# Four places in a hand-written TensorE order: two weighted sums and two heads' output transposes in an attention stage

## The chip, the cores and the metric

The kernel runs on one core of a Trainium2 chip. The metric is the device time of one execution in microseconds. Runs of the kernel before took 1316.26 to 1317.3 us, with a median of 1317.28.

## What is computed

The program is a two-layer decoder trunk for 512 tokens of width 1024, all in float32: a Mamba-2 mixer and a convolutional feed-forward layer, then differential attention and another feed-forward layer. The change is in the attention, whose reference is, cut to the core:

```
def block(args):
    qblk, i = args
    ...
    logits = jnp.einsum('bqhcd,bkhcd->bhcqk', qblk, k).astype(jnp.float32) * scale
    logits = logits + bias[None, :, None]
    logits = jnp.where(dist >= 0, logits, -jnp.inf)
    p = jax.nn.softmax(logits, axis=-1)
    attn = p[:, :, 0] - lam * p[:, :, 1]
    return jnp.einsum('bhqk,bkhd->bqhd', attn.astype(v.dtype), v)
...
o = rms_norm(o, subln_g) * (1.0 - lam_init)
return o.reshape(b, s, V_TOTAL) @ out_w
```

There are 8 heads. Each head has two query and key maps of 64 features (c = 0, 1) and one value of 128. The output of each head is normalised over its 128 features, and all heads go through one output projection.

## The kernel before

Every projection has its operands split into a rounded high half and a remainder, and three matmuls (high by high, high by low, low by high) make one product. The helper `mm3` (lines 207 to 210) does this for the output projection; `proj` (lines 1326 to 1349) does it for values and queries. Weights come by DMA, two pieces ahead of their use; ScalarE makes the high half (`wh`) and VectorE the low half (`wl`, line 174 or 159).

**Units.** Attention works in units (class `Unit`, line 1499). A head has three units, `PARTS`: query blocks 0 and 1, query block 2, query block 3, because of the causal mask. Units are numbered head_part, as in 4_0. Four operations make up the work on a unit:

- `logits` (lines 1509 to 1541): TensorE makes the logits of both maps into two PSUM banks; VectorE adds the bias and finds the row's extreme (line 1533) and so frees the bank; ScalarE takes the exponential (line 1540).
- `weigh` (lines 1543 to 1552): VectorE combines the two maps into one set of weights (line 1550).
- `turn` (lines 1554 to 1560): TensorE transposes the weights (line 1559), and ScalarE copies them out of PSUM (`at`, line 1560).
- `values` (lines 1562 to 1574): TensorE makes the weighted sum of the values (`po`, line 1570), with the transposed weights as the stationary operand, and ScalarE copies the result to `ot` (line 1573). After a head's last unit follows `normed_out` (lines 1576 to 1586): a square on ScalarE, a sum, a reciprocal root and the multiplication at line 1586 on VectorE.

A head that is normalised goes through `turned_out` (lines 1588 to 1599): four transposes on TensorE (`oT`, line 1592), a ScalarE copy that makes the high half (`oh`, line 1596) and a VectorE operation that makes the low half (`ol`, line 1597). The bank is free when both have read it.

**Banks.** PSUM has two pools of four banks. Logits, turned weights, weighted sums, output transposes and the transposes of queries (`ktq`, copied out as `qT` on ScalarE, line 1375) share the pool `aux`; projections use the pool `mm`.

**Order.** Only TensorE's order is written by hand (line 1647 opens a manual schedule for it). It is a list of strings, `ORDER` (line 1484), one row for each pair of units, read by the loop at lines 1687 to 1695:

- L: logits and weighing of the next pair of units
- f: the next step of a filler, a chain of generators (line 1653): values of heads 0 to 3, queries of heads 4 to 7, values of heads 4 to 7, then the first half of the output projection. Each has 16 steps of six matmuls with 512 columns, and ten of these steps run ahead of the list.
- a: `turn` of the next unit; v: `values` of the next unit; o: `turned_out` of the next normalised head

The order of instructions on ScalarE and VectorE is laid by the framework when the program is built. Each engine then runs its own in that order. One example of where this order differs from the code's: the normalising multiplications of the second query projection (`knq`, line 1361) are kept back by the code until the filler step f35.

Counted from zero, these are the steps around the change, as the list has them before:

```
row 4   L4(2_2,3_0) f31 f32 a7(2_1) v6(2_0) f33 v7(2_1) f34 o1 a8(2_2) f35
row 5   L5(3_1,3_2) f36 f37 a9(3_0) v8(2_2) f38 v9(3_0) a10(3_1) f39
row 7   L7(4_2,5_0) f44 f45 a13(4_1) f46 v12(4_0) f47 o3 a14(4_2) f48
row 8   L8(5_1,5_2) f49 f50 v13(4_1) a15(5_0) f51 v14(4_2) v15(5_0) a16(5_1)
row 10  L10(6_2,7_0) f56 f57 a19(6_1) v18(6_0) f58 v19(6_1) o5 a20(6_2)
row 11  L11(7_1,7_2) f59 f60 a21(7_0) v20(6_2) f61 v21(7_0) a22(7_1)
```

The steps f32 to f47 make the values of heads 4 to 7, token block by token block within each pair of input blocks. The copies of the finished values (`vt`, line 1480) are issued by f45 for the token blocks 0 and 1 and by f47 for the blocks 2 and 3. The transposes of the queries follow f36 and f37. The output projection's first half begins with f48.

After the list `last_out` (line 1627) does the last head's transposes and the second half of the output projection, and the second feed-forward layer (line 1699) follows.

Of the kernel before, what the change touches and what calls it, by code (L numbers as in the profile page):

```python
# [42 lines left out]
def trunk_kernel(ctx: ExitStack, tc, x, ssm_ln_g, ssm_in_w, ssm_conv_w, ssm_conv_b, ssm_dt_bias,  # L43
# [1249 lines left out]
    with tc.tile_pool(name="att", bufs=1) as ap, ExitStack() as later:  # L1293
# [184 lines left out]
        def vproj(key, i):  # L1478
            def evac(b, ps, rt):
# [17 lines left out]
        fl = lambda a: a.rearrange("p a b -> p (a b)")  # L1497
# [238 lines left out]
```

## Time and profile before

| What | Value |
|---|---|
| Runs | 1316.26, 1317.28, 1317.3 us |
| Profiled execution | 1317.05 us |
| Its span, first to last instruction | 1315.3 us |
| Mean granted TensorE clock | 1.000 |
| HBM traffic | 160.21 MB read, 6.44 MB written |

The profile names engines PE (TensorE matmuls), PEld (TensorE weight loads, which overlap PE), DVE (VectorE), ACT (ScalarE), POOL and SP. Times are microseconds from the span's start. In the timeline a row has the start, the duration, the engine, the line of the kernel, the operation, `out<-in` by tile names, the shape and a count; a square bracket has the idle time of the engine ahead of it and what ended that. Several like instructions in a row are merged into one. A float32 matmul whose operands aren't split shows as two instructions, so a weighted sum of three products shows as x6. The list of waits gives, for each pair of waiter and releaser, the total, the count and the longest. The attention stage with the list runs from about 803 to 940 us.

### The profile page before, as it was taken

What the parts mean: (1) busy time and instruction counts of PE and PEld (TensorE: products, weight loads), DVE (VectorE), ACT (ScalarE), POOL (GpSimd) and SP (SyncE); (2) the same over time, 40 slices, a digit from 0 to 9 for tenths busy, and PEclk for the clock granted to TensorE, in tenths of its full rate; (3) what the DMA queues carried; (4) which work ended last, traced back from release to release, by engine and by line L of the source; (5) the groups of instructions that cost most, each with busy time, mean ns of one, the idle gap of its engine ahead of it and who ended that gap; (6) DMA issues with size and microseconds to landing.
All of it is one profiled execution on the core that took longest, in us unless ns stands there. A gap on an engine that the chain in (4) does not pass through costs nothing.

```text
span 1315.3 us, 18265 instructions
## 1 busy us (share of the span) xinstructions
PE 1307.8 (99%) x6771; PEld 1096.2 (83%) x6771; DVE 1073.1 (82%) x1774; ACT 713.8 (54%) x1156; POOL 176.8 (13%) x244
## 2 busy tenths in 40 slices
PE   9999999999999999999999999999999999999998
PEld 8878888888888988898889887777888888888887
DVE  7989878888888877876888878677777978887886
ACT  6696554743344445544556667676654444544452
POOL 5230200300021401020113210000020100010001
PEclk9999999999999999999999999999999999999999
DMA  7453433432234657673766754222224445443635
GB/s 210 150 162 88 150 101 109 138 95 87 82 96 138 124 142 203 180 161 113 216 168 145 192 128 120 73 65 66 64 80 160 98 118 186 103 96 112 192 64 128
DMA packets 202552, 167.84 MB, mean 128 GB/s; under 512 B 7580, under 2 KB 175904, under 8 KB 202464
## 3 DMA queue, kind: packets, MB, share of 16 engines
q1 hardware_dynamic: 176080, 124.93, 31.8%
q0 software_dynamic: 22928, 36.46, 14.7%
q10 hardware_dynamic: 3456, 5.30, 1.1%
q8 instruction: 53, 0.87, 0.3%
q14 instruction: 35, 0.29, 0.1%
HBM read 160.21 MB, written 6.44 MB: 127 GB/s over the span
## 4 chain that ended last, share of the span: by engine, by line
PE 98%; ACT 1%; DVE 1%; issue 0%; DVEq 0%
PE ps_g L209 6%; PE ps_u L210 6%; PE ps_g L210 6%; PE ps_u L209 6%; PE ps_u L208 6%; PE ps_g L208 6%; PE ps_in L208 5%; PE ps_in L210 5%; PE ps_in L209 5%; PE ps_s L1239 3%; PE ps_s L1244 3%; PE ps_s L1242 3%; PE ps_s L1146 3%; PE ps_s L1141 3%; PE ps_s L1144 3%; PE ps_o L209 2%
## 5 line engine op out<-in xcount | busy, mean ns | idle before, releaser
L208 PE MATMUL ps_u<-xgh,wh_u 128*128 128x512 f32 x352 | 137.4, 390 | 0.0
L209 PE MATMUL ps_g<-xgl,wh_g 128*128 128x512 f32 x352 | 137.2, 390 | 0.0
L208 PE MATMUL ps_g<-xgh,wh_g 128*128 128x512 f32 x352 | 137.0, 389 | 0.0
L210 PE MATMUL ps_u<-xgh,wl_u 128*128 128x512 f32 x352 | 137.0, 389 | 0.0
L210 PE MATMUL ps_g<-xgh,wl_g 128*128 128x512 f32 x352 | 137.0, 389 | 0.0
L209 PE MATMUL ps_u<-xgl,wh_u 128*128 128x512 f32 x352 | 136.9, 389 | 0.0
L208 PE MATMUL ps_in<-xgh,wh_in 128*128 128x512 f32 x304 | 122.9, 404 | 0.0
L210 PE MATMUL ps_in<-xgh,wl_in 128*128 128x512 f32 x304 | 119.7, 394 | 0.0
L209 PE MATMUL ps_in<-xgl,wh_in 128*128 128x512 f32 x304 | 119.2, 392 | 0.0
L209 PEld LDWEIGHTS ps_g<-xgl,wh_g 128*128 128x128 f32 x352 | 66.0, 188 | 14.3 <-DVE xgl L488 0.7
L1244 PE MATMUL ps_s<-sl,wh_s 128*128 128x256 f32 x308 | 77.5, 283 | 0.0
L1242 PE MATMUL ps_s<-sh,wh_s 128*128 128x256 f32 x308 | 77.5, 283 | 0.0
L210 PEld LDWEIGHTS ps_g<-xgh,wl_g 128*128 128x128 f32 x352 | 66.1, 188 | 13.7
L209 PEld LDWEIGHTS ps_u<-xgl,wh_u 128*128 128x128 f32 x352 | 66.1, 188 | 13.6
L210 PEld LDWEIGHTS ps_u<-xgh,wl_u 128*128 128x128 f32 x352 | 66.0, 188 | 13.7
L208 PEld LDWEIGHTS ps_g<-xgh,wh_g 128*128 128x128 f32 x352 | 66.1, 188 | 13.6
L208 PEld LDWEIGHTS ps_u<-xgh,wh_u 128*128 128x128 f32 x352 | 66.1, 188 | 13.6
L1126 ACT ACTIVATE sh<-vg 128x256 fp32r<-128x256 f32 (+1 forms) x44 | 23.1, 524 | 99.1 <-DVE vg L1276 99.1
L1052 POOL DMA_DIRECT2D wz<-in_ffn_down_w_dram x36 | 44.2, 1290 | 235.2 <-DVE wl_s L1080 163.1
L1272 ACT ACTIVATE vg<-vg 128x512 f32<-128x512 f32 x44 | 27.8, 632 | 78.4 <-DVE vg L1024 78.3
L1024 DVE SCALAR_TENSOR_TENSOR vg<-ug,cf,vg 128x511 f32<-128x511 f32 x88 | 65.8, 747 | 5.5 <-ACT vg L1022 4.1
L1024 DVE SCALAR_TENSOR_TENSOR vu<-uu,cf,vu 128x511 f32<-128x511 f32 x88 | 65.7, 747 | 2.8 <-ACT vu L1022 1.4
(425 smaller groups left out, 3465.0 us busy)
## 6 DMA issues: line engine op xcount, KB each, us to landing
wr_g<-in_ffn_up_w_dram SPq DMA_DIRECT2D x44, 512.0 KB, 3.9
wr_u<-in_ffn_up_w_dram SPq DMA_DIRECT2D x44, 512.0 KB, 3.9
wr_in<-in_ssm_in_w_dram SPq DMA_DIRECT2D x40, 512.0 KB, 3.9
wz<-in_ffn_down_w_dram POOLq DMA_DIRECT2D x27, 512.0 KB, 5.8
m<-cumd POOLq DMA_DIRECT2D x16, 512.0 KB, 4.7
wr_out<-in_ssm_out_w_dram SPq DMA_DIRECT2D x16, 512.0 KB, 3.5
wr_s<-in_ffn_down_w_dram SPq DMA_DIRECT2D x13, 512.0 KB, 3.9
xT<-in_ffn_down_w_dram SPq DMA_DIRECT2D x10, 512.0 KB, 7.2
```

The source lines that it names most:

```text
L208: pe.matmul(ps, wh, xh, start=start, stop=False)
L209: pe.matmul(ps, wh, xl, start=False, stop=False)
L210: return pe.matmul(ps, wl, xh, start=False, stop=stop).ins
L1024: dve.scalar_tensor_tensor(out=v[:, s:], in0=u[:, :T - s], scalar=col(2 - s), in1=v[:, s:], op0=ALU.mult, op1=ALU.add)
L1052: pool.dma_start(view(t, nq), source(p0, c, nq, j, i), accum_op=ALU.add)
L1141: pe.matmul(pss[b], h, ws[q][1][:, cols], start=False, stop=end and q == qs[-1], skip_group_check=more)
L1144: pe.matmul(pss[b], h, ws[q][0][:, cols], start=first and q == qs[0], stop=False, skip_group_check=more)
L1146: pe.matmul(pss[b], w, ws[q][0][:, cols], start=False, stop=False, skip_group_check=more)
L1239: pe.matmul(v[:, b], wl[:, q, cols], h, start=False, stop=q == nq - 1, skip_group_check=not opens or b > 0)
L1242: pe.matmul(v[:, b], wh[:, q, cols], h, start=opens and q + b == 0, stop=False, skip_group_check=not opens or b > 0)
L1244: pe.matmul(v[:, b], wh[:, q, cols], w, start=False, stop=False, skip_group_check=not opens or b > 0)
L1272: act.activation(ga, ga, AF.Silu)
```

## The change

Three rows of the list differ, in four places. In row 4 the weighted sum v7 stands behind f34 instead of ahead of it. In row 7 the weighted sum v12 stands behind f47, and head 3's output transposes o3 stand ahead of f47. In row 10 head 5's output transposes o5 stand ahead of f58 and v19. The same steps are done in every row, and no operation is added or removed.

```
-                 "L f f a v f v f o a f",
+                 "L f f a v f f v o a f",
                  "L f f a v f v a f",
                  "L f f a v f v o a f",
-                 "L f f a f v f o a f",
+                 "L f f a f o f v a f",
                  "L f f v a f v v a",
                  "L f f a v f v o a f",
-                 "L f f a v f v o a",
+                 "L f f a v o f v a",
                  "L f f a v f v a",
                  "f a v f o v")
```

## The prediction

> **What bounds the kernel now.** The page comes first: the busy shares and the chain of work that ended last.
>
> ```profile
> PE 1307.8 (99%) x6771; PEld 1096.2 (83%) x6771; DVE 1073.1 (82%) x1774; ACT 713.8 (54%) x1156; POOL 176.8 (13%) x244
> PE 98%; ACT 1%; DVE 1%; issue 0%; DVEq 0%
> ```
>
> TensorE holds 98% of the chain. A place in its order is worth something only where it waits, so the next views are its busy time in stretches of the attention stage, and its own waits between 800 and 950 us.
>
> ```profile
> 840.00:860.00 20.00, 18.63 (x107) 14.48 (x106) 15.55 (x52) 16.39 (x45) 0.00 (x0) 1.00 0.22 66
> 860.00:880.00 20.00, 19.65 (x115) 15.38 (x116) 14.97 (x49) 14.63 (x40) 0.00 (x0) 1.00 0.22 66
> 880.00:900.00 20.00, 19.35 (x109) 14.66 (x108) 12.69 (x38) 13.23 (x33) 0.00 (x0) 1.00 0.20 67
> PE po L1570 <- ACT at L1560: 1.7, 1, 1.7
> PE po L1570 <- ACT vt L1480: 0.7, 1, 0.7
> ```
>
> The columns of a stretch are its start and end, its length, then PE, PEld, DVE, ACT and POOL busy, the granted clock and the DMA load. The clock is 1.00 throughout. TensorE has two holes, both in front of weighted sums (po, line 1570): one waits for a ScalarE copy of turned weights (at, line 1560), one for a ScalarE copy of values (vt, line 1480). To place them among the steps I read the timeline. Counting in the fixed list, I number the steps from zero: f34 is the 35th fill step, v7 the eighth weighted sum, o1 the second head's output transposes, a8 the ninth turn, L5 the sixth pair of logits.
>
> **The change, part by part.** Fill steps here are six matmuls of 512 columns; a weighted sum is a few matmuls and one ScalarE copy; an output transpose is four transposes, a ScalarE copy (oh) and a VectorE subtraction (ol). The fill steps that change places issue no DMA, and f47 alone has copies behind it (two of vt). So nothing moves past a DMA in SP's or POOL's queue.
>
> First, f34 ahead of v7.
>
> ```profile
> 857.00 0.47 PE L1335 MATMUL ps_v<-wh_v,xgh 128*128 128x512 f32 x1
> 858.24 0.40 PE L1337 MATMUL ps_v<-wh_v,xgl 128*128 128x512 f32 x1
> 859.83 0.47 ACT L1560 ACTIVATE at<-at 128x384 f32<-128x384 f32 x1
> 860.35 0.94 PE L1570 MATMUL po<-vt,at 128*128 128x128 f32 x6 [1.72 <-ACT at L1560]
> 861.04 0.48 PE L1335 MATMUL ps_v<-wh_v,xgh 128*128 128x512 f32 x1
> 862.52 0.60 PE L1592 MATMUL oT<-ident,ot 128*128 128x128 f32 x4
> ```
>
> f33 runs from 857.00, v7 at 860.35, f34 from 861.04, o1 at 862.52. A fill step takes 862.52 - 861.04 = 1.48 us, so v7 could have started at 857.00 + 1.48 = 858.48 and waits 1.87. The copy it waits for ends at 860.30 and stands in ScalarE's queue, which the edit leaves alone ahead of v7. With f34 in the hole TensorE is busy until 857.00 + 2.96 = 859.96, v7 still starts at 860.35, takes 861.04 - 860.35 = 0.69, and o1 follows at 861.04: **1.48 us earlier**. The upper end is 1.87, if that copy came earlier too.
>
> [...]
>
> What is late next? Behind o1 come a8, f35 and L5, and these rows set the pace:
>
> ```profile
> 862.43 1.89 DVE L1361 TENSOR_TENSOR knq<-knq,ssq 128x512 f32<-128x512 f32 x3
> 863.16 0.69 ACT L1596 ACTIVATE oh<-oT,c 128x512 fp32r<-128x512 f32 x1 [1.44 <-PE oT L1592]
> 864.24 0.74 DVE L1597 SCALAR_TENSOR_TENSOR ol<-oT,c,oh 128x512 fp32r<-128x512 f32 x1
> 864.88 1.77 PE L1527 MATMUL lg<-kT,qT 64*128 64x384 f32 x8
> 866.59 0.50 PE L1335 MATMUL ps_v<-wh_v,xgh 128*128 128x512 f32 x1
> 865.83 0.56 DVE L1533 CUSTOM_DVE_ANT_0 lg<-lg,tb 128x384 f32<-128x384 f32 x1 [0.17 <-PE lg L1527]
> 866.31 0.75 DVE L174 SCALAR_TENSOR_TENSOR wl_v<-wr_v,c,wh_v 128x512 fp32r<-128x512 f32 x1
> 868.06 0.75 DVE L174 SCALAR_TENSOR_TENSOR wl_v<-wr_v,c,wh_v 128x512 fp32r<-128x512 f32 x1
> 868.73 0.68 DVE L1533 CUSTOM_DVE_ANT_0 lg<-lg,tb 128x512 f32<-128x512 f32 x1
> 866.43 0.62 ACT L1540 ACTIVATE lg<-lg,mx 128x384 f32<-128x384 f32 x1
> 869.45 0.72 ACT L1540 ACTIVATE lg<-lg,mx 128x512 f32<-128x512 f32 x1 [0.46 <-DVE mx L1533]
> 870.17 2.40 ACT L1375 ACTIVATE qT<-ktq,c 128x512 f32<-128x512 f32 x4
> 871.58 0.61 PE L1570 MATMUL po<-vt,at 128*128 128x128 f32 x4
> ```
>
> VectorE is full from 862.43, with query multiplications (knq, line 1361) whose start no edit moves. Two things hang on its order, which the build lays and the old trace only hints at. (a) o1's bank is freed by ol. New, oh would run from 861.04 + 0.64 = 861.68 to 862.37 (0.64 is 863.16 - 862.52), so ol can start at 862.4, level with the first knq. L5 would start at 863.40; the third of its four banks, asked for 768 of 1792 columns in (0.73 of its 1.71 us, an estimate), is wanted at 864.13. With ol first or second on VectorE it is free by 863.8 and costs nothing; with ol still behind three knq it ends at 864.98 and costs 0.85. (b) L5's four reductions (line 1533) now have two weight subtractions of 0.75 among them, since a bank was not full yet when VectorE asked. New, all four are ready when VectorE is done with ol and four knq (2.52 + 0.74, near 865.6). Taken back to back they end near 867.9 instead of 869.41; the four exponentials (0.62, 0.62, 0.72, 0.72) then end near 868.9 instead of 870.17, the second of the four qT copies (0.6 each) near 870.1 instead of 871.4. v8 takes that copy's bank and has only 0.2 us to spare now (871.58 against 871.4); it would start near 870.2, **1.38 us earlier**. If both subtractions stay where they are, the reductions end only 0.2 earlier and v8 0.35. The code issues L5's reductions ahead of those subtractions, so I take 1.38; ends 0.35 and 1.87.
>
> Second, o3 and then f47 ahead of v12.
>
> ```profile
> 890.32 0.68 DVE L1586 TENSOR_TENSOR ot<-ot,so 128x512 f32<-128x512 f32 x1
> 892.66 0.61 PE L1570 MATMUL po<-vt,at 128*128 128x128 f32 x4
> 893.19 0.67 ACT L1480 ACTIVATE vt<-ps_v,tr_nkv 128x512 f32<-128x512 f32 x1
> 893.92 0.49 PE L1570 MATMUL po<-vt,at 128*128 128x128 f32 x2 [0.65 <-ACT vt L1480]
> 894.16 0.47 PE L1335 MATMUL ps_v<-wh_v,xgh 128*128 128x512 f32 x1
> 895.63 0.60 PE L1592 MATMUL oT<-ident,ot 128*128 128x128 f32 x4
> 896.42 0.48 PE L208 MATMUL ps_ao<-oh,wh_ao 128*128 128x512 f32 x1
> 921.88 0.83 PE L1570 MATMUL po<-vt,at 128*128 128x128 f32 x6
> 922.47 0.47 PE L208 MATMUL ps_ao<-oh,wh_ao 128*128 128x512 f32 x1
> ```
>
> Now v12, f47, o3 and a14 take 896.42 - 892.66 = 3.76. Without a wait they take: v12 0.59 (a sum of the same shape, 922.47 - 921.88), f47 895.63 - 894.16 = 1.47, o3 and a14 together 896.42 - 895.63 = 0.79: 2.85, a gain of **0.9**. Is the wait really gone? v12 would start near 892.66 + 0.44 + 1.47 = 894.57 (0.44 for o3 is an estimate, over half of the 0.79); the copy it needs ends at 893.86, and at 894.55 if o3's own copy (0.69, as above) went ahead of it on ScalarE. Both are in time. o3 needs head 3 normalised, which ends at 891.00, 1.66 before 892.66. Behind the moved v12, ScalarE's ot copy and a14 come later than the vt copies, and have f48 and L8 as cover. Ends: 0 and 0.9; it is nearest to the upper, since both producers are done.
>
> Third, o5 ahead of f58 and v19, with a20 left next to L11.
>
> ```profile
> 920.74 0.69 DVE L1586 TENSOR_TENSOR ot<-ot,so 128x512 f32<-128x512 f32 x1
> 925.58 2.32 PE L1527 MATMUL lg<-kT,qT 64*128 64x384 f32 x8
> 925.97 0.75 DVE L1597 SCALAR_TENSOR_TENSOR ol<-oT,c,oh 128x512 fp32r<-128x512 f32 x1 [0.96 <-ACT oh L1596]
> 927.83 0.50 PE L208 MATMUL ps_ao<-oh,wh_ao 128*128 128x512 f32 x1
> ```
>
> L11 takes 927.83 - 925.58 = 2.25, where L5, with the same four tiles, takes 866.59 - 864.88 = 1.71: 0.54 lost inside a step that the list of waits shows as busy, because a bank is held until ol ends at 926.72 and ScalarE's at copy stands behind o5's oh. Moved, o5 starts at 922.47, its oh and ol are done before 925.58, and the **0.54** goes; ends 0 and 0.54. o5's own input is ready at 921.43, 1.04 ahead.
>
> The sum: 1.38 + 0.9 + 0.54 = 2.8 us. Later stages have TensorE alone in the chain, so I carry it to the end. The profiled execution took 1317.05 us (span 1315.3); less 2.8 that is 1314.25. The median of the runs shown, 1317.28, lies 0.23 above it, so the forecast is **1314.5**. About 0.2% (2.6 us) is what a measurement of this kernel can tell from no change, and the sum stands just above it.
>
> **The rivals.** *VectorE's order stays* (0.22): the subtractions remain between L5's reductions and v8 waits for the qT copy; the first edit leaves 0.35, the sum is 1.8, the time 1315.5. For it: v8's 0.2 us of margin. Against it: VectorE ran ol, which was ready at 863.85, right after the knq it was then in, so its order follows readiness. *The waits move on* (0.12): copies are laid anew on ScalarE, and one edit pays while the others are taken back behind it; about 0.7, 1316.6. This includes a v12 that waits as before. *The copy comes earlier* (0.09): ScalarE's at for v7 moves up and the first edit gives 1.87; 3.3, 1314.0. *The early transposes wait* (0.07), the slower case: head 3's and head 5's normalisations run late, and o3 and o5, which now stand ahead of fill steps, hold TensorE. If they come L us later relative to TensorE than now, that costs (L - 1.66) + (L - 1.04); from L = 2.75 it eats the whole 2.8, at 3.0 it gives 1317.8, and from 4.1 it is slower by over 0.2%. Against it: that needs four more VectorE operations of 0.75 ahead of each.
>
> **How the numbers follow.** The forecast has 0.50. Its own spread is about 2.2 to 3.2 us, and some seven tenths of it lies above 2.6; with the earlier copy that makes faster 0.35 + 0.09 = 0.44. Slower is the tail of the last rival, 0.04; the rest, 0.52, is no change that can be told. The range runs from 1313.6, past the earlier copy, to 1316.6, through the two smaller gains; the forecast alone would have 1314.1 to 1315.1. Beyond it lie the slower case and half of the case that moves on.
>
> **What would show it.** After the change: no wait over 0.6 us at v7, o1 directly behind it; L5 at its 1.71; the two wl_v subtractions behind the last of L5's reductions; v8 1.2 to 1.5 earlier against f33; v12 without a hole in the middle; L11 at 1.7. It is wrong if v8, o3 or o5 shows a new wait, or if the PE busy time from 840 to 900 still lacks over 1 us.

## The result, and the profile after

The changed kernel took **1314.61 us** (median; 1313.80 to 1315.50) beside 1316.91 us of the kernel before on the same chip: a ratio of 0.9981, 95% interval 0.9975 to 0.9987, 2.30 us by the medians. Timed once more, beside another set of runs of the kernel before, it was 1314.82 against 1316.63, a ratio of 0.9986 (0.9977 to 0.9994), or 1.81 us. The forecast was 1314.5, with a sum of 2.8 us and a range from 1313.6 to 1316.6. The profiled execution took 1314.37 us with a span of 1312.7. Two executions of the experiments below took 1867.12 us (e2_row7) and 2663.43 us (e5_o1_first); the ratios leave them out, the medians hold them.

First the chain on the page of the changed kernel.

```profile
PE 99%; ACT 1%; DVE 0%; issue 0%; DVEq 0%
```

Then the three stretches of the attention stage, with the columns as before (start:end, length, PE, PEld, DVE, ACT, POOL, clock, DMA), and TensorE's own waits from 780 to 950 us, of which one is left.

```profile
840.00:860.00 20.00, 19.73 (x112) 15.46 (x112) 15.83 (x53) 16.68 (x46) 0.00 (x0) 1.00 0.20 65
860.00:880.00 20.00, 19.93 (x119) 15.65 (x120) 15.91 (x52) 15.00 (x42) 0.00 (x0) 1.00 0.22 66
880.00:900.00 20.00, 20.00 (x111) 15.34 (x111) 14.00 (x44) 14.68 (x37) 0.00 (x0) 1.00 0.28 93
```

```profile
PE po L1570 <- ACT at L1560: 0.3, 1, 0.3
```

TensorE is busy for 59.66 of these 60 us; before it was 57.63. The clock is 1.00 in both, so the 2.03 us are holes that closed. The third edit lies outside the window, at 920 us, and closes lost time inside a step.

The two profiled executions don't stand at the same place when the first edit comes: f33 starts at 856.72 here and at 857.00 before. So I measure from f33, which no edit moves, to o7, the last head's transposes behind the list (943.93 before, 941.23 after): 86.93 against 84.51, **2.42 us** gained inside the stage.

Now the three places. The timeline of the changed kernel around the first edit:

```profile
856.72 0.47 PE L1335 MATMUL ps_v<-wh_v,xgh 128*128 128x512 f32 x1
860.07 0.94 PE L1570 MATMUL po<-vt,at 128*128 128x128 f32 x6 [0.35 <-ACT at L1560]
860.85 0.60 PE L1592 MATMUL oT<-ident,ot 128*128 128x128 f32 x4
861.88 1.29 DVE L1361 TENSOR_TENSOR knq<-knq,ssq 128x512 f32<-128x512 f32 x2
863.10 0.74 DVE L1597 SCALAR_TENSOR_TENSOR ol<-oT,c,oh 128x512 fp32r<-128x512 f32 x1
863.21 1.81 PE L1527 MATMUL lg<-kT,qT 64*128 64x384 f32 x8
864.95 0.50 PE L1335 MATMUL ps_v<-wh_v,xgh 128*128 128x512 f32 x1
865.91 0.74 DVE L174 SCALAR_TENSOR_TENSOR wl_v<-wr_v,c,wh_v 128x512 fp32r<-128x512 f32 x1
867.19 0.68 DVE L1533 CUSTOM_DVE_ANT_0 lg<-lg,tb 128x512 f32<-128x512 f32 x1
867.87 0.73 DVE L174 SCALAR_TENSOR_TENSOR wl_v<-wr_v,c,wh_v 128x512 fp32r<-128x512 f32 x1
868.73 2.39 ACT L1375 ACTIVATE qT<-ktq,c 128x512 f32<-128x512 f32 x4
870.03 0.97 PEld L1570 LDWEIGHTS po<-vt,at 128*128 128x128 f32 x8 [0.21 <-ACT qT L1375]
870.03 1.16 PE L1570 MATMUL po<-vt,at 128*128 128x128 f32 x8
870.94 0.47 PE L1335 MATMUL ps_v<-wh_v,xgh 128*128 128x512 f32 x1
```

v7 is 3.35 behind f33, as before: its copy did not come earlier, and 0.35 of the wait is left. o1 follows v7 by 0.78, where before it came 2.17 behind (862.52 less 860.35): **1.39** gained. L5 takes 1.74 (1.71 before) and ol was laid in front of the third knq, so the bank of o1 costs next to nothing. One of the two weight subtractions stays among L5's reductions (865.91), the other went behind the last of them (867.87). The first knq starts 861.88 - 856.72 = 5.16 behind f33; before it was 862.43 - 857.00 = 5.43. The reason lies on ScalarE, where the second step of the reciprocal root that knq needs (ssq, line 500) stood behind v7's copy (line 1573). In the kernel before:

```profile
861.32 0.28 ACT L1573 ACTIVATE ot<-po 128x128 f32<-128x128 f32 x1
861.50 0.22 ACT L500 ACTIVATE ssq<-ssq 128x32 f32<-128x32 f32 x1
```

In the changed kernel it stands ahead of that copy, which starts at 861.08:

```profile
860.94 0.23 ACT L500 ACTIVATE ssq<-ssq 128x32 f32<-128x32 f32 x1
```

v8 is released by the second qT copy (868.73, two copies of 0.6), and its weights load only then, at the same moment as its first matmul; before, they were 0.11 ahead. The list of TensorE's waits doesn't show this one. v8 stands 870.03 - 856.72 = 13.31 behind f33, before 871.58 - 857.00 = 14.58: 1.27. The step after it, f38, stands 870.94 - 856.72 = 14.22 behind f33, and stood 15.39 behind it in the kernel before, by this row of its timeline:

```profile
872.39 0.48 PE L1335 MATMUL ps_v<-wh_v,xgh 128*128 128x512 f32 x1
```

So **1.17** leaves this place. The second edit, in the timeline of the changed kernel:

```profile
888.86 0.68 DVE L1586 TENSOR_TENSOR ot<-ot,so 128x512 f32<-128x512 f32 x1
891.20 0.60 PE L1592 MATMUL oT<-ident,ot 128*128 128x128 f32 x4
891.74 0.68 ACT L1480 ACTIVATE vt<-ps_v,tr_nkv 128x512 f32<-128x512 f32 x1
893.02 0.83 PE L1570 MATMUL po<-vt,at 128*128 128x128 f32 x6
893.97 0.75 DVE L1597 SCALAR_TENSOR_TENSOR ol<-oT,c,oh 128x512 fp32r<-128x512 f32 x1 [0.89 <-ACT oh L1596]
894.04 0.47 PE L208 MATMUL ps_ao<-oh,wh_ao 128*128 128x512 f32 x1
895.61 1.79 PE L1527 MATMUL lg<-kT,qT 64*128 64x384 f32 x8
```

v12 shows as one step of six matmuls without a hole; the copy it needs is done at 892.42. The four steps from o3 to f48 take 894.04 - 891.20 = 2.84, forecast 2.85, before 3.76. o3 starts 1.66 behind the end of its normalisation (889.54). ol3 ends at 894.72, ahead of L8 at 895.61. The third edit:

```profile
922.62 0.74 DVE L1597 SCALAR_TENSOR_TENSOR ol<-oT,c,oh 128x512 fp32r<-128x512 f32 x1
923.27 1.92 PE L1527 MATMUL lg<-kT,qT 64*128 64x384 f32 x8
925.12 0.50 PE L208 MATMUL ps_ao<-oh,wh_ao 128*128 128x512 f32 x1
```

L11 takes 925.12 - 923.27 = 1.85, before 2.25, forecast 1.7: **0.40** gained. ol ends at 923.36, 0.09 after L11 has begun: its oh is done at 922.06, but VectorE has been in two weighings (line 1550) since 921.95 and comes to ol only at 922.62. What that does inside the step is seen in the view of line 1527 over its first 0.25 us (columns: count; shortest, median and longest in ns; starts of the first and the last). First L5, then L11.

```profile
L1527 PE MATMUL lg<-kT,qT x2: 587/587/587, 863.2 to 863.2; 64*128 64x384 f32 x2
```

```profile
L1527 PE MATMUL lg<-kT,qT x2: 587/587/587, 923.3 to 923.4; 64*128 64x384 f32 x2
```

In L5 the matmuls of the two maps start together (each uses 64 of the rows); in L11 the second map starts 0.15 later (923.42 in the trace, against 923.27), when ol has given back its bank, and stays behind to the end. That is the 0.14 that is missing to 0.54.

### The profile page after: what moved, and what is told of

Read it like the earlier page. It is cut to its first block, busy times and chain, and to the rows that moved or that the text cites. A ratio compares the mean times of both kernels' runs of the same rounds, so it can differ in the third digit from the quotient of the medians.

```text
span 1312.7 us, 18264 instructions
## 1 busy us (share of the span) xinstructions
PE 1307.3 (100%) x6771; PEld 1096.3 (84%) x6771; DVE 1073.9 (82%) x1774; ACT 713.9 (54%) x1156; POOL 177.1 (13%) x244
## 4 chain that ended last, share of the span: by engine, by line
PE 99%; ACT 1%; DVE 0%; issue 0%; DVEq 0%
PE ps_g L209 6%; PE ps_u L208 6%; PE ps_g L208 6%; PE ps_u L210 6%; PE ps_g L210 6%; PE ps_u L209 6%; PE ps_in L208 5%; PE ps_in L210 5%; PE ps_in L209 5%; PE ps_s L1239 3%; PE ps_s L1244 3%; PE ps_s L1242 3%; PE ps_s L1146 3%; PE ps_s L1141 3%; PE ps_s L1144 3%; PE ps_o L209 2%
## 5 line engine op out<-in xcount | busy, mean ns | idle before, releaser
L1021 DVE TENSOR_TENSOR uu<-ps_u,nr_f 128x512 f32<-128x512 f32 x44 | 30.4, 690 | 48.0 <-PE ps_u L210 48.0
```

What stands on the lines that cost most here:

```text
L1021: dve.tensor_tensor(out=u, in0=ps, in1=r, op=ALU.mult)
```

## The experiments

All distances are from f33 to o7 in the profiled execution; the medians stand beside runs of the kernel before on the same chip.

| Kernel | f33 | o7 | Distance | Against before | Median, before's | Ratio (95%) |
|---|---|---|---|---|---|---|
| before | 857.00 | 943.93 | 86.93 | | | |
| changed | 856.72 | 941.23 | 84.51 | -2.42 | 1314.61, 1316.91 | 0.9981 (0.9975 to 0.9987) |
| e1_row4 | 856.31 | 942.11 | 85.80 | -1.13 | 1315.88, 1316.79 | 0.9993 (0.9984 to 1.0002) |
| e2_row7 | 856.25 | 942.30 | 86.05 | -0.88 | 1316.04, 1316.79 | 0.9992 (0.9983 to 1.0001) |
| e3_row10 | 857.73 | 944.27 | 86.54 | -0.39 | 1316.67, 1316.79 | 0.9998 (0.9989 to 1.0007) |
| e4_sum_only | 856.46 | 943.12 | 86.66 | -0.27 | 1316.85, 1316.79 | 0.9998 (0.9989 to 1.0007) |
| e5_o1_first | 856.91 | 941.43 | 84.52 | -2.41 | 1314.43, 1317.07 | 0.9980 (0.9971 to 0.9988) |
| e6_a20_first | 856.87 | 941.40 | 84.53 | -2.40 | 1314.07, 1317.07 | 0.9978 (0.9969 to 0.9986) |
| e7_o3_early | 857.45 | 946.35 | 88.90 | +1.97 | 1319.14, 1317.07 | 1.0013 (1.0004 to 1.0021) |
| e8_knq_pool | 857.16 | 942.33 | 85.17 | -1.76 | 1315.34, 1317.07 | 0.9987 (0.9978 to 0.9995) |
| e10_changed_again | 856.42 | 940.90 | 84.48 | -2.45 | 1314.82, 1316.63 | 0.9986 (0.9977 to 0.9994) |
| e11_a20_again | 857.42 | 941.95 | 84.53 | -2.40 | 1314.62, 1316.63 | 0.9982 (0.9973 to 0.9991) |

**Each row alone.** The theory: the three edits are worth what each is worth alone. The rival: one pays, and the others only move its wait.

```
e1   -"L f f a v f v f o a f"   +"L f f a v f f v o a f"     (row 4)
e2   -"L f f a f v f o a f"     +"L f f a f o f v a f"       (row 7)
e3   -"L f f a v f v o a"       +"L f f a v o f v a"         (row 10)
```

> Only v7 behind f34 (row 4); the other two rows as before. Theory (each edit removes its own wait, and what it gains is carried to the end by TensorE alone): v7 still waits, 0.3 to 0.5 us instead of 1.7; o1 is 1.4 us earlier than in the kernel before, v8 1.2 earlier since it then waits for the bank that the second qT copy frees, and 1.2 stays to the end: the time falls by 1.2 us. The hole in v12 stays 0.8. Rival (the edits pay only together): the gain is taken back at the hole in v12, which grows to 2.0, and the time is that of the kernel before.

> Only row 7: o3 ahead of f47, v12 behind it. Theory: v12 runs without a hole, f48 starts 0.86 us earlier than in the kernel before, the 1.7 wait at v7 stays, and the time falls by 0.9 us. Rival (the edits pay only together): without the earlier start that row 4's edit gives, ScalarE is as far behind at this place and v12 waits for the values all the same; under 0.3 us.

> Only row 10: o5 ahead of f58 and v19. Theory: L11 takes 1.85 us instead of 2.25 since its bank no longer waits for ol, and the rest up to 1.71 is the wait for the copy of a20 right ahead of it; a21 starts 0.4 us earlier than in the kernel before; the time falls by 0.4 us. Rival (a20 alone holds L11): nothing, L11 stays at 2.25.

The distances are 1.13, 0.88 and 0.39 shorter, together 2.40 of the 2.42. The waits of TensorE show it too: with row 4 alone the wait at v12 stands untouched beside the rest of v7's,

```profile
PE po L1570 <- ACT vt L1480: 0.7, 1, 0.7
PE po L1570 <- ACT at L1560: 0.3, 1, 0.3
```

and with row 7 alone the wait at v7 does:

```profile
PE po L1570 <- ACT at L1560: 1.7, 1, 1.7
```

The edits are independent, and the rival falls. In e3_row10 L11 takes 1.85, as expected; whether the rest is a20's copy, as the expectation has it, is tried further down. Each alone is too small for the runs (every interval holds 1); the traces tell.

**Row 7 with v12 moved and o3 left behind it.** Is o3's move needed, or only v12's? The other rows are those of the kernel before.

```
-"L f f a f v f o a f"
+"L f f a f f v o a f"
```

> Row 7 with v12 behind f47 but o3 left behind v12, where it was: the place of the weighted sum alone. Theory: f47 by itself covers the wait (v12 would start 1.4 us later than in the kernel before, 0.2 us after the values' copy ends), o3's move is worth nothing here, f48 0.86 us earlier as with both, time 0.9 less. Rival: the 0.2 us is too little, since ScalarE's copies are laid anew; v12 keeps a hole of 0.3 to 0.5 and the gain is 0.4 to 0.6.

The kernel was 0.27 better than the kernel before, not 0.88, and neither theory gave that. v12 has no hole here either, but the timeline shows what came in its place:

```profile
894.71 1.06 ACT L148 ACTIVATE wh_ao<-wr_ao 128x1024 fp32r<-128x1024 f32 x1
896.48 2.38 PE L1527 MATMUL lg<-kT,qT 64*128 64x384 f32 x8
896.94 0.74 DVE L1597 SCALAR_TENSOR_TENSOR ol<-oT,c,oh 128x512 fp32r<-128x512 f32 x1
897.74 0.29 PEld L1527 LDWEIGHTS lg<-kT,qT 64*128 64x128 f32 x2 [0.29 <-DVE ol L1597]
898.79 0.50 PE L208 MATMUL ps_ao<-oh,wh_ao 128*128 128x512 f32 x1
```

o3 now comes as late as 894.12. A weight copy of 1.06 us (wh_ao) is laid ahead of its oh on ScalarE, and on VectorE the subtraction that belongs to that copy (line 159, 1.23 us from 895.80) is laid ahead of its ol. So ol ends only at 897.68, 1.2 after L8 has begun; L8 waits for that bank and takes 898.79 - 896.48 = 2.31 where the changed kernel's takes 1.71 (897.32, the start of f49 there, less 895.61). In the changed kernel ol3 ended 0.9 ahead of L8 (894.72 against 895.61). So o3's move is worth 0.6 of the second edit's 0.88: it gives the bank back in time. This is the rival of waits that move on, in one edit left half done.

**o1 ahead of v7.** 0.35 of v7's wait is left; o1 could fill it.

```
-"L f f a v f f v o a f"
+"L f f a v f f o v a f"     (row 4 of the changed kernel)
```

> The changed kernel, with o1 ahead of v7 too (row 4: f33 f34 o1 v7), to fill the 0.35 us that v7 still waits. Theory (past v7 it is VectorE's query multiplications, then the qT copies on ScalarE, that set v8): L5 starts 0.4 to 0.5 us earlier than in the changed kernel, v8 at most 0.2 earlier, the time moves by 0.0 to 0.2. Rival (TensorE's order alone sets the pace): v8 and everything behind it 0.4 to 0.5 earlier, time 0.45 less.

In the trace L5 starts 6.05 behind f33 (862.96), in the changed kernel 6.49 (863.21), as the theory had it. Then come, in its timeline:

```profile
868.93 2.40 ACT L1375 ACTIVATE qT<-ktq,c 128x512 f32<-128x512 f32 x4
870.22 0.97 PEld L1570 LDWEIGHTS po<-vt,at 128*128 128x128 f32 x8 [0.26 <-ACT qT L1375]
```

v8 loads its weights 870.22 - 856.91 = 13.31 behind f33, to the hundredth where it does in the changed kernel. The qT copies start 12.02 behind f33 in this kernel and 12.01 in the changed one. v7's last wait is worth nothing: behind it the chain knq, reductions, exponentials, qT copies sets the time, and moving TensorE's steps ahead of it doesn't move it (the first knq is 5.17 behind f33 here, 5.16 in the changed kernel).

**a20 ahead of v19.** Can L11 come down to 1.7?

```
-"L f f a v o f v a"
+"L f f a v o f a v"     (row 10 of the changed kernel)
```

> The changed kernel, with a20 ahead of v19 (row 10: o5 f58 a20 v19), so that a weighted sum stands between a20 and L11. Theory (L11's remaining 0.14 us is the wait for the copy of a20's bank): L11 takes 1.71 us, a21 is 0.14 earlier, the time is 0.1 less, which only the trace can show. Rival (some bank is always late by so much, whichever step stands last): v19's copy holds L11 in its place, 1.85 or more.

> The changed kernel once more, as the neighbour of the next run. Theory: 2.4 us of gain in the trace, so a median 1.9 to 2.6 us under the kernel before.

> The changed kernel with a20 ahead of v19 in row 10, timed beside the changed kernel. Theory: its trace ended where the changed kernel's did (2.41 against 2.43 us early), so the 0.5 us by which its median was lower does not come back: the two medians lie within 0.4 us of each other. Rival: the places are worth 0.5 us that one profiled execution did not show; its median is again 0.4 us or more lower.

In the trace of the first run:

```profile
922.79 0.74 DVE L1597 SCALAR_TENSOR_TENSOR ol<-oT,c,oh 128x512 fp32r<-128x512 f32 x1
923.45 1.91 PE L1527 MATMUL lg<-kT,qT 64*128 64x384 f32 x8
925.29 0.50 PE L208 MATMUL ps_ao<-oh,wh_ao 128*128 128x512 f32 x1
```

L11 takes 1.84 again: ol ends at 923.53, 0.08 behind L11's start. So it is ol that holds L11, neither a20's copy nor v19's, and the reason given for the rest of L11 in e3_row10's expectation was wrong. The distance is the changed kernel's within 0.02. Its median had come out 0.5 lower, though, so the two were timed side by side, and there they are 0.20 apart (1314.82 and 1314.62), with intervals that overlap for the most part. No kernel of this study beats the changed one by what the runs can tell.

**o3 two fill steps too early.** What does a wait of early transposes, the slower rival, cost?

```
-"L f f a f o f v a f"
+"L o f f a f f v a f"     (row 7 of the changed kernel)
```

> The changed kernel with o3 too early: right behind L7, ahead of f44 (row 7: L o f f a f f v a f). It measures the slower case: transposes that wait for their own normalisation. Theory: in the changed kernel head 3 is normalised at 889.5 and o3 would be asked for at 886.6, so TensorE waits 2.9 us there; v12 has no hole; all else shifts; 2.9 us over the changed kernel, 0.6 over the kernel before. Rival (the normalisation is laid earlier when its reader stands earlier): it moves ahead of L7's reductions on VectorE, the wait is 1 to 2 us, the time 1 to 2 over the changed kernel.

The wait came as expected, 2.91 us, and the kernel lost more: 88.90 - 84.51 = 4.39 against the changed one. Its timeline, and the windows with the granted clock in the third column from the end:

```profile
890.34 1.12 PE L1592 MATMUL oT<-ident,ot 128*128 128x128 f32 x4 [2.91 <-DVE ot L1586]
892.11 0.63 PE L1337 MATMUL ps_v<-wh_v,xgl 128*128 128x512 f32 x1
892.53 0.63 PE L1335 MATMUL ps_v<-wh_v,xgh 128*128 128x512 f32 x1
893.93 0.39 PE L1336 MATMUL ps_v<-wl_v,xgh 128*128 128x512 f32 x1
894.16 0.40 PE L1337 MATMUL ps_v<-wh_v,xgl 128*128 128x512 f32 x1
```

```profile
890.30:892.00 1.70, 1.66 (x6) 1.57 (x7) 1.17 (x8) 1.23 (x5) 0.00 (x0) 0.50 1.03 340
892.00:893.60 1.60, 1.60 (x5) 1.21 (x5) 1.39 (x3) 1.16 (x5) 0.00 (x0) 0.51 0.22 76
```

Around the end of the wait the granted clock is 0.50 for about 3.4 us. This is an estimate, worked out from three windows: 0.94 from 889.0 to 890.3, then the two shown; it is 1.00 again from 893.6 to 895.0. A matmul follows the last one after 0.42 (892.53 less 892.11) instead of 0.23 (894.16 less 893.93). From o3's start at 890.34 some 3.2 us are left at half the clock, which do the work of 1.6 (an estimate): this is where the other 1.48 us went. In the kernel before, the wait at v7 (1.72 on its row) had no such drop behind it: the clock was 1.00 from 840 to 900 us. The drop does not come in every execution, it seems: of eleven runs the nine with a mean clock of 0.998 or 0.999 took 1318.03 to 1319.60 us, and the two with 1.000 took 1316.70 and 1317.42. The wait alone would give about 1317.3, e5_o1_first's median and 2.91. The times say this more surely than the means do: e3_row10's profiled execution has a mean of 0.999 too, and 1.00 in each of the three stretches from 840 to 900 us.

**Two of the four knq on GpSimd.** If VectorE's chain holds v8, taking two multiplications off it should free v8's last 0.2.

```
-dve.tensor_tensor(out=v, in0=v, in1=ss[:, b, :].unsqueeze(2).to_broadcast([P, 8, 64]),
+(pool if key == "q1" and b > 1 else dve).tensor_tensor(out=v, in0=v, in1=ss[:, b, :].unsqueeze(2).to_broadcast([P, 8, 64]),
```

> The changed kernel, with two of the four query multiplications (knq, line 1361, blocks 2 and 3 of the second projection) on GpSimd instead of VectorE. It takes 1.25 us from VectorE ahead of L5's reductions. Theory (VectorE's queue there is what v8 waits for in the end): L5's reductions start 0.8 us or more earlier, the qT copies follow, v8 waits for nothing and is 0.2 earlier against o1, time 0.2 less. Rival (ScalarE's copies are late by themselves): reductions earlier, v8 not. If GpSimd is slow (over 2 us each), ktq for blocks 2 and 3 waits instead and the kernel is slower.

The stage was 0.66 longer than the changed kernel's (85.17 against 84.51). The view of the tile knq (ns: shortest, median, longest) and the timeline:

```profile
L1361 DVE TENSOR_TENSOR knq<-knq,ssq x2: 693/1112/1531, 862.3 to 862.9; 128x512 f32<-128x512 f32 x2
L1361 POOL TENSOR_TENSOR knq<-knq,ssq x2: 1445/1462/1478, 862.5 to 863.9; 128x512 f32<-128x512 f32 x2
```

```profile
863.65 2.66 PE L1527 MATMUL lg<-kT,qT 64*128 64x384 f32 x8
865.18 0.29 PEld L1527 LDWEIGHTS lg<-kT,qT 64*128 64x128 f32 x2 [0.60 <-DVE ol L1597]
866.24 0.50 PE L1335 MATMUL ps_v<-wh_v,xgh 128*128 128x512 f32 x1
```

VectorE's second knq, from 862.9, took 1531 ns, while GpSimd was in its own two (862.5 to 865.4); the first, from 862.3, took 693, and in the changed kernel, with all of them on VectorE, none took more than 694. So ol ended only at 865.13, L5 waited for its bank and took 866.24 - 863.65 = 2.59. v8 lost its wait, but L5 had lost 0.85 by then. The prediction gave the same figure for an ol behind three knq; that they agree so closely is chance. VectorE was not relieved: its reductions start 8.15 behind f33 (865.31), in the changed kernel 8.24 (864.96). So neither the theory nor its rival was tried, and what a shorter queue on VectorE would do for v8 stays open. The theory had not counted on a longer knq, and what makes it longer was not shown.

## Why the prediction was right, and where its sizes were off

The direction, the places and the range were right; the sum was too large, 2.8 against 2.42 in the trace and 2.30 and 1.81 by the medians. That the forecast time was met within 0.1 owes something to the reference: it was taken from a median of 1317.28, and the kernel before came out at 1316.91 beside the changed one. With that reference the same sum would have given 1314.1. About 0.2% was named as the edge of what can be told; the result, 0.19%, stands on it.

- *First edit*, forecast 1.38, measured 1.17. v7 started as foreseen. The 1.48 at o1 was 1.39: the step v7 takes 0.78 in front of transposes, and 0.69 was its length in front of a fill step. At v8 two errors of the forecast offset one another. It had VectorE lay both subtractions behind L5's reductions, and one stayed among them; and it took the start of knq for something that no edit moves, which came 0.27 earlier against f33. The reductions began 8.24 behind f33 for a forecast of 8.6, so the last of them ended only about 0.25 late (11.15 for 10.9), and v8 lost 0.12 more to the qT copy. That the start of v8 came out so near is in part luck. A further 0.10 is v8's weight load, which began with v8's first matmul (870.03) and had begun 0.11 ahead of it in the kernel before. This is also, in small, one of the signs of being wrong that the prediction named, a new wait at v8 (0.21 on its weight load). The rival in which VectorE's order stays was thus half true in its mechanism and wrong in its price: it gave 0.35 for this edit. e5_o1_first shows that the qT copies are what sets v8. Why one subtraction stayed was not tried; a bank that wasn't full yet, the reason given for the old order, does not fit this execution, since L5's matmuls had ended at 865.02, 0.89 ahead of it.
- *Second edit*, forecast 0.9, measured 0.92 on its four steps (2.84 after, 3.76 before) and 0.88 at o7 when made alone. Their forecast was 2.85, and o3 was 1.66 behind its input, as worked out. The step that the prediction left thin is what o3's move is for: it named f48 and L8 as cover for the copies behind v12, and e4_sum_only shows that L8 is no cover but the next to wait, if o3 stays.
- *Third edit*, forecast 0.54, measured 0.40. "Its oh and ol are done before L11" failed by 0.09 us: ol ended at 923.36, L11 began at 923.27, since VectorE did weighings first. One bank of four came 0.15 late, and the step took 0.14 more than L5's 1.71 in the kernel before.
- *The earlier copy* did not come: v7 stands 3.35 behind f33 in both. *Waits that move on* are out for the change as made, by the sum of the three rows alone.
- *The slower rival* did not happen, but its price was wrong. It counted a wait at its length; in e7_o3_early a wait of 2.91 cost 4.39, with the granted clock at 0.50 behind it. A wait between 1.72 and 2.91 us was not tried, and what brings the clock down was not shown.

## What to carry to other kernels

Moving independent work into a wait is worth the wait only up to the next thing that is not set by that engine: follow the buffers that the moved steps hold (here the banks of o1, o3 and o5) and ask who asks for them next, since half of an edit can hand its gain to the following step. A late bank is not seen in the list of waits when it lies inside a step of several matmuls (L11's 2.25 in the kernel before, where the list has only the waits at v7 and v12); compare the step's length with that of its equals (L5's 1.71). When a move carries a step toward its input, a long wait on TensorE can cost more than its length: here 2.91 us cost 4.39.

## What the runs showed of the hardware

- After a wait of 2.91 us in e7_o3_early TensorE ran at half the granted clock for some 3.2 us, of about 3.4 at that clock (estimates, from 0.94, 0.50 and 0.51 in three windows); after the wait of 1.72 at v7 in the kernel before it was 1.00.
- In e8_knq_pool a VectorE multiplication knq took 1531 ns while GpSimd was in the same operation; the one before it, which GpSimd's overlapped in its last 0.5 us, took 693, and those of the changed kernel 678 to 694. GpSimd took 1445 and 1478 ns.
